# A depthwise convolution recast in eight token phases: full-width matmuls, weights spread by ScalarE, and conv tiles dealt out between GLU pieces

## The chip, the cores and the metric

The kernel runs on all 8 NeuronCores of one Trainium2 chip, two dies of four cores (0 to 3 and 4 to 7). Each core computes half the tokens of one of four batch items; the cores don't exchange data. The metric is the device time in microseconds (us) of the slowest core.

PE is TensorE (matmuls), PEld its weight loads, DVE VectorE, ACT ScalarE, POOL GpSimd, SP SyncE (here only a queue that issues DMAs).

## The reference, cut to what matters

```python
z = rms_norm(h, g_mix) @ w_in            # (B, T, 5*1024), T = 4096 + 16 meta tokens
# y_conv: the branch that the change is about
a = z[..., :1024] * sigmoid(z[..., 1024:2048])        # GLU
a = depthwise_conv(a, w_dw, width=31, centred) + b_dw # one 31-tap filter per channel
y_conv = silu(layer_norm(a, ln_g, ln_b)) @ w_conv_out # LayerNorm over all 1024 channels
# y_pool: centred window means (2, 4, 8, 16 tokens) minus the token, two matmuls
h = h + (gateA * y_conv + gateB * y_pool) @ w_o
h = h + swiglu(rms_norm(h, g_ffn))                    # 1024 -> 2816 -> 1024
out = rms_norm(h, g_final)
```

A depthwise convolution mixes tokens within a channel, whereas the conv matmuls of both kernels sum over 128 partitions (`ps<-rep_186,cw_187 128*32` in the trace of before). So both kernels bring several tokens of one channel onto different partitions. They do that by writing the GLU product to DRAM and reading it back in another arrangement.

## The kernel before

The conv stage handles 8 chunks of 128 channels. Each chunk's GLU is a pass `vg(c)` of 5 pieces of 416 tokens. The order of the passes is what the argument is about:

```python
def vg(c):                                  # one GLU pass: 80 matmuls
    for p in range(NPC):                    # NPC = 5 pieces of PW = 416 tokens
        ...                                 # 8 matmuls "gate", 8 matmuls "val"
        act(s_, bg_[:, 0:PW], AF.Sigmoid)
        tt(DVE, aT[c % 2][:, sl], bv[:, 0:PW], s_, ALU.mult)     # the GLU product
        if p == 2:
            a_out(c, 0, 3 * PW)             # SBUF -> DRAM "ad"
        pump(2)                             # two steps of the window means, on VectorE
    a_out(c, 3 * PW, EXT)

def im2col(c):                              # DRAM "ad" -> SBUF "rep": 8 loads, 4 shifted copies
    ...

def conv(c):                                # 4 tiles of 512 tokens
    for b in range(NB):
        for q in range(8):
            for j in range(4):              # 32 channels at a time, in a quarter of the array
                ...matmul(o, lhsT=lt, rhs=r_, tile_position=(0, 32 * j))
        act(d_sb[c][b][:], ps[:], AF.Identity, bias=pcc(PC_BDW, c))   # stays in SBUF
        act(dq, ps[:], AF.Square, bias=pcc(PC_BDW, c))
        ...                                 # VectorE adds to the LayerNorm sums acc_s, acc_q
    if c + 2 < KC:
        build_cw(c + 2)                     # GpSimd: the conv weights as diagonal blocks

vg(0)
im2col(0)
for c in range(1, KC):
    vg(c)
    conv(c - 1)                             # one whole GLU pass after its products
    im2col(c)
```

`nb()` hands out PSUM banks in turn, `S.dma` and `S.op` insert the semaphore waits that the data needs, and `pump(n)` issues n pieces of background work. After the loop come the gate matmuls `A(0, b)`, `conv(7)`, the LayerNorm statistics and then the rest of the block, which the change leaves alone but for the order of the tokens.

Of the kernel before, what the change touches and what calls it, by code (L numbers as in the profile page):

```python
# [13 lines left out]
KC = 8  # L14
# [9 lines left out]
HALO = 15  # L24
# [10 lines left out]
HW_ = TOK // 2  # L35
RW = HW_ + 28
RWP = 1056
THIRDS = ((0, 683), (683, 683), (1366, 682))
S_W = 704
# [5 lines left out]
(PC_BGA, PC_BGB, PC_BDW, PC_LNG, PC_LNB, PC_PSC, PC_GMIX, PC_GFFN, PC_GFIN) = range(0, 72, 8)  # L45
PC_WDW = 72
PC_COLS = PC_WDW + KC * 4 * 8
# [17 lines left out]
class Sched:  # L65
# [9 lines left out]
    def gran(self, ap):  # L75
# [17 lines left out]
        for (s, c) in dims[:-1]:  # L93
            if s == 0 or c == 1:
                continue
            offs = [o + i * s * esz for o in offs for i in range(c)]
        gs = set()
# [95 lines left out]
def build_nc():  # L193
# [18 lines left out]
    em_d = din("emask", [128, 32], BF16)  # L212
    out_d = nc.dram_tensor("out", [NB, 128, KC * TT], F32, kind="ExternalOutput")
    h1_d = nc.dram_tensor("h1d", [NB, 128, KC * TT], F32, kind="Internal")
    a_d = nc.dram_tensor("ad", [KC, 128, EXT], BF16, kind="Internal")
# [21 lines left out]
    def alloc(name, shape, dt):  # L237
# [5 lines left out]
    emask = alloc("emask_s", [128, 32], BF16)  # L243
# [10 lines left out]

    uT = at("uT", [128, KC, EXT], BF16, oA)
    psb = [at(f"psb{c}", [128, EXT], F32, oB + c * EXT * 4) for c in range(KC)]

    sqx = at("sqx", [128, KC, EXT], F32, oB)
    mT = at("mT", [128, KC, TOK], BF16, oM)
    slot = [at(f"wslot{i}", [128, 1024], BF16, oS + i * 2048) for i in range(NSLOT)]  # L260
# [3 lines left out]
    d_sb = [[at(f"d{c}_{b}", [128, TT], F32, oB + c * EXT * 4 + b * 2048) for b in range(NB)]  # L264
            for c in range(KC)]
# [4 lines left out]
    acc_s = at("acc_s", [128, TOK], F32, oW)  # L270
    acc_q = at("acc_q", [128, TOK], F32, oW + 8192)
# [7 lines left out]
    z = oZ  # L279
    aT = [at(f"aT{i}", [128, EXT], BF16, z + i * EXT * 2) for i in range(2)]  # L280
    z += 2 * EXT * 2
    rep = [at(f"rep{i}", [128, 4, RWP], BF16, z + i * 4 * RWP * 2) for i in range(2)]
    z += 2 * 4 * RWP * 2
    cw = [at(f"cw{i}", [128, 4, 8, 32], BF16, z + i * 2048) for i in range(2)]
    z += 4096
    sg = [at(f"sg{i}", [128, PW], F32, z + i * PW * 4) for i in range(2)]
    z += 2 * PW * 4
    dsq = [at(f"dsq{i}", [128, TT], F32, z + i * 2048) for i in range(2)]
    z += 4096
    s1 = at("s1", [128, S_W], F32, z)  # L290
    s2 = at("s2", [128, S_W], F32, z + S_W * 4)
    z += 2 * S_W * 4
    assert z <= oZ + NZT * 2048, (z - oZ, NZT * 2048)
# [50 lines left out]
    ad_sem = [dsem(f"d_ad{i}") for i in range(2)]  # L344
# [116 lines left out]
    for (o, i_) in ((invc[:], ic_d.ap()), (emask[:], em_d.ap())):  # L461
        S.dma(SP, cst, o, i_, val=32)
# [85 lines left out]
    def windows(c):  # L548
        g = c // 2
        wd = WINS[g]  # L550
        out = []
        for ti, (t0, n) in enumerate(THIRDS):
            lo = t0 + HALO - wd // 2
            width = n + wd - 1
            step, tgl = 1, 0
            src = psb[c][:, lo:lo + width]
            while step < wd:
                nw = width - step
                dst = (s1, s2)[tgl][:, 0:nw]
                out.append(lambda dst=dst, a=src[:, 0:nw], b=src[:, step:step + nw]:  # L560
                           tt(DVE, dst, a, b, ALU.add))
                src, width = dst, nw
                step *= 2
                tgl ^= 1
            assert width == n

            def fin(src=src, t0=t0, n=n, ti=ti):
                stt(DVE, mT[:, c, t0:t0 + n], src, 1.0 / wd, psb[c][:, HALO + t0:HALO + t0 + n],
                    ALU.mult, ALU.subtract)
                if ti == 2:  # L570
                    tt(DVE, tmp8[:], src[:, n - 8:n], invc[:, g * 8:(g + 1) * 8], ALU.mult)
                    tt(DVE, mT[:, c, TOK - 8:TOK], tmp8[:],
                       psb[c][:, HALO + TOK - 8:HALO + TOK], ALU.subtract)
                    win_done.add(c)
            out.append(fin)
        return out
# [4 lines left out]
    def build_cw(c):  # L581
        o = cw[c % 2][:].rearrange("p j q m -> p (j q) m")
        i0 = emask[:].unsqueeze(1).to_broadcast([128, 32, 32])
        ws = pc[:, PC_WDW + c * 32:PC_WDW + (c + 1) * 32]
        i1 = ws.unsqueeze(2).to_broadcast([128, 32, 32])
        S.op(POOL, lambda e: e.tensor_tensor(out=o, in0=i0, in1=i1, op=ALU.mult), [emask[:], ws], [o])

    def vg(c):
        for p in range(NPC):
            sl = slice(p * PW, (p + 1) * PW)  # L590
            bv, bg_ = nb(), nb()
            for k in range(KC):
                mm(bg_[:, 0:PW], w(f"gate{c}", k), uT[:, k, sl], k == 0, k == KC - 1)
            for k in range(KC):
                mm(bv[:, 0:PW], w(f"val{c}", k), uT[:, k, sl], k == 0, k == KC - 1)
            s_ = sg[p % 2][:]
            act(s_, bg_[:, 0:PW], AF.Sigmoid)
            tt(DVE, aT[c % 2][:, sl], bv[:, 0:PW], s_, ALU.mult)
            if p == 2:
                a_out(c, 0, 3 * PW)  # L600
            pump(2)
        a_out(c, 3 * PW, EXT)
        release(f"gate{c}", f"val{c}")

    def a_out(c, lo, hi):
        h = 0 if lo == 0 else 1
        S.dma(SP, ad_sem[h], a_d.ap()[c][:, lo:hi], aT[c % 2][:, lo:hi], xw=[("ad", c, h)])

    def im2col(c):
        for h in range(2):  # L610
            S.wait_prod(SP, ad_sem[h])
            tot = rep_sem[h].count + 16 * 4
            for s_ in range(4):
                src = a_d.ap()[c].rearrange("(j i) t -> i j t", j=4)[:, :, HW_ * h + s_:HW_ * h + s_ + RW]
                S.dma(SP, rep_sem[h], rep[h][32 * s_:32 * s_ + 32, :, 0:RW], src, val=tot)

    def conv(c):
        pump_until(win_done, c)
        for b in range(NB):
            h = b // 2  # L620
            ps = nb()
            for q in range(8):
                for j in range(4):
                    o = ps[32 * j:32 * j + 32, :]
                    lt = cw[c % 2][:, j, q, :]
                    x0 = (b % 2) * TT + 4 * q
                    r_ = rep[h][:, j, x0:x0 + TT]
                    S.op(PE, lambda e, o=o, lt=lt, r_=r_, q=q, j=j: e.matmul(  # L628
                        o, lhsT=lt, rhs=r_, start=(q == 0), stop=(q == 7), tile_position=(0, 32 * j)),
                        [lt, r_], [o], signal=(q == 7 and j == 3))  # L630
            act(d_sb[c][b][:], ps[:], AF.Identity, bias=pcc(PC_BDW, c))
            tok = slice(b * TT, (b + 1) * TT)
            dq = acc_q[:, tok] if c == 0 else dsq[b % 2][:]
            act(dq, ps[:], AF.Square, bias=pcc(PC_BDW, c))
            if c == 1:
                tt(DVE, acc_s[:, tok], d_sb[0][b][:], d_sb[1][b][:], ALU.add)
            elif c > 1:
                tt(DVE, acc_s[:, tok], acc_s[:, tok], d_sb[c][b][:], ALU.add)
            if c > 0:
                tt(DVE, acc_q[:, tok], acc_q[:, tok], dq, ALU.add)  # L640
            pump(1)
        if c + 2 < KC:
            build_cw(c + 2)

    build_cw(0)
    build_cw(1)
    vg(0)
    im2col(0)
    for c in range(1, KC):
        vg(c)  # L650
        conv(c - 1)
        im2col(c)
# [7 lines left out]
    def tile_mm(wname, rhs, weff_c=None):  # L660
        b = nb()
        for k in range(KC):
            lhsT = w(wname, k) if weff_c is None else weff[:, k, weff_c * 128:(weff_c + 1) * 128]
            mm(b[:], lhsT, rhs(k), k == 0, k == KC - 1)
        return b

    def u_rhs(b):
        return lambda k: uT[:, k, HALO + b * TT:HALO + (b + 1) * TT]

# [3 lines left out]
    def A(c, b):  # L673
        ps = tile_mm(f"gA{c}", u_rhs(b))
# [3 lines left out]
    def Bm(c, b):  # L678
        ps = tile_mm(f"gB{c}", u_rhs(b))
# [19 lines left out]
    zorder = list(range(NZT - 3, NZT)) + list(range(NZT - 3))  # L699
# [5 lines left out]
    conv(7)  # L705
# [4 lines left out]
    def ln_stat(b):  # L710
        tok = slice(b * TT, (b + 1) * TT)
# [4 lines left out]
        mm(pm[:], ones[:], acc_s[:, tok], True, True)  # L716
        mm(pq[:], ones[:], acc_q[:, tok], True, True)
        if b == NB - 1:
            var, mean, rstd = acc_q[:, tok], pm[:], psum[7][:]
# [54 lines left out]

    for g in range(4):
        wps_scale(g)
    for b in range(NB):
        A(1, b)
# [215 lines left out]
def _host_inputs(inputs):  # L994
# [12 lines left out]
    for col, v in ((PC_BGA, bg[:D]), (PC_BGB, bg[D:]), (PC_BDW, arr("b_dw")), (PC_LNG, arr("ln_g")),  # L1007
                   (PC_LNB, arr("ln_b")), (PC_PSC, arr("pool_scale")), (PC_GMIX, arr("g_mix")),
                   (PC_GFFN, arr("g_ffn")), (PC_GFIN, np.asarray(inputs["g_final"], f32))):
        pc[:, col:col + 8] = fm(v)  # L1010
    wpad = np.concatenate([arr("w_dw"), np.zeros((1, D), f32)], 0)

    pc[:, PC_WDW:] = wpad.reshape(8, 4, KC, 4, 32).transpose(1, 4, 2, 3, 0).reshape(128, KC * 32)
    emask = np.zeros((128, 32), ml_dtypes.bfloat16)
    for s_ in range(4):
# [64 lines left out]
```

## Time and profile before

| | before |
|---|---|
| time, median of its runs | 1033.8 us (1033.4 to 1035.4) |
| PE busy | 1005.6 us, 97% of the slowest core's span |
| VectorE, ScalarE, GpSimd busy | 450, 308, 158 us |
| a chunk in the conv stage | 21.2 us: 14.17 GLU, 7.02 conv |
| PE's waits for the reloaded products | 2.3 us in all |

The profiled execution itself took 1041.3 us: in it the four cores of die 1 ran at a mean clock of 0.986 to 0.990, those of die 0 at 0.995 to 0.997.

From the page of the kernel before, which is that of core 7, its slowest: the busy sums, the granted TensorE clock in tenths over 40 slices of the span, and the chain of waits that ended last, by engine. The last line is from PE's waits on the same core (total us, times, longest).

```profile
PE 1005.6 (97%) x5696; PEld 489.7 (47%) x5696; DVE 450.1 (43%) x693; ACT 307.6 (30%) x500; POOL 158.0 (15%) x182
...
PEclk9999999999989999999999999999999999999999
...
PE 91%; DMA 4%; DVE 2%; ACT 1%; issue 1%; SPq 0%; POOL 0%; DVEq 0%; ACTq 0%; POOLq 0%
...
PE ps L628 <- DMA rep_186<-ad: 2.3, 2, 1.7
```

PE is busy nearly always, and the chain that ended last runs through PE for 91% of the span. This kernel is bound by TensorE.

Two chunks of its conv stage on core 2. The columns are named in the first line; PEclk is the share of the full clock that was granted.

```profile
core 2: us, PE busy (x) PEld busy (x) DVE busy (x) ACT busy (x) POOL busy (x), PEclk, DMA share, GB/s
149.50:170.70 21.20, 21.20 (x210) 11.09 (x209) 20.38 (x30) 7.67 (x14) 6.49 (x4) 1.00 0.70 151
170.70:191.90 21.20, 21.20 (x210) 11.08 (x209) 20.41 (x30) 7.67 (x14) 6.49 (x4) 1.00 0.73 154
```

PE has work for all 21.2 us of a chunk, at full clock, and VectorE is nearly full as well (20.4 of 21.2 us).

How long the way through DRAM takes shows best in the chain of waits in order of time (core 7): start, duration, engine or DMA, what it wrote and read.

```profile
106.51 0.60 DVE aT_183 L367
107.18 6.51 DMA ad<-aT_183
...
115.09 9.29 DMA rep_186<-ad
...
124.63 3.64 PE ps L628 x64
128.27 14.17 PE ps L353 x80
142.44 7.02 PE ps L628 x128
```

After the last product of chunk 0, made by 107.1 us, the write takes 6.5 us, the reload 9.3, and its conv may start at 124.6: 17.5 us later. That costs nearly nothing, since a GLU pass of 14.17 us stands in between, and the convolution of later chunks is 21 us behind its products.

### The profile page before, as it was taken

How to read it: one execution, taken by the hardware profiler on the slowest of the kernel's cores; microseconds unless marked ns; L12 is line 12 of the kernel's file. 1: busy time of each engine (PE TensorE's matmuls, PEld its weight loads, DVE VectorE, ACT ScalarE, POOL GpSimd, SP SyncE). 2: the span in 40 equal slices, each digit the busy share in tenths (PEclk: the TensorE clock that was granted, in tenths of full speed). 3: DMA queues.
4: the chain of work that ended last, by engine and by line, in shares of the span. 5: the costliest groups of instructions: out<-in, count | busy, mean ns of one | idle time of the engine just before them, and what ended most of it. 6: DMA issues, size and time to landing. Idle time of an engine off the chain costs nothing.

```text
span 1039.7 us, 15674 instructions; the slowest of 8 cores (1026.0 to 1039.7 us)
## 1 busy us (share of the span) xinstructions
PE 1005.6 (97%) x5696; PEld 489.7 (47%) x5696; DVE 450.1 (43%) x693; ACT 307.6 (30%) x500; POOL 158.0 (15%) x182
## 2 busy tenths in 40 slices
PE   3899999999999999999999999999999999999997
PEld 1645555555434444444444444444444444444486
DVE  4542789974278532233546521212121221342454
ACT  2643333343487612211144311111111111121121
POOL 2143122221420000000167001111000000000000
PEclk9999999999989999999999999999999999999999
DMA  9705876667254111111887446655222202403112
GB/s 215 212 1 94 177 165 145 149 155 157 50 88 65 31 31 31 31 21 21 209 317 154 100 79 96 95 85 83 35 35 34 32 1 92 151 39 124 81 82 82
DMA packets 34251, 99.90 MB, mean 96 GB/s; under 512 B 3968, under 2 KB 7168, under 8 KB 31616
## 3 DMA queue, kind: packets, MB, share of 16 engines
q0 software_dynamic: 17888, 45.10, 24.6%
q1 hardware_dynamic: 16288, 53.81, 17.8%
q8 instruction: 47, 0.77, 0.3%
q14 instruction: 28, 0.23, 0.1%
HBM read 111.93 MB, written 21.04 MB: 128 GB/s over the span
## 4 chain that ended last, share of the span: by engine, by line
PE 91%; DMA 4%; DVE 2%; ACT 1%; issue 1%; SPq 0%; POOL 0%; DVEq 0%; ACTq 0%; POOLq 0%
PE ps L353 86%; PE ps L628 5%; DMA rep_186<-ad 2%; DMA xb_178<-xp 1%; DVE uT L374 1%; DMA ad<-aT_183 1%; DVE sqx L367 1%; DMA wslot_68<-w_pool_out 0%; ACT sqx L364 0%; ACT ps L364 0%; DVE h2b_259 L374 0%; ACT L364 0%; SPq L190 0%; ACT zt_197 L364 0%; ACT zt_203 L364 0%
## 5 line engine op out<-in xcount | busy, mean ns | idle before, releaser
L353 PE MATMUL ps<-mT,weff 128*128 128x512 bf16 x256 | 60.7, 386 | 0.0
L353 PE MATMUL ps<-uT,wslot_60 128*128 128x512 bf16 (+6 forms) x224 | 51.8, 356 | 5.9 <-DVE uT L374 5.3
L353 PE MATMUL ps<-uT,wslot_65 128*128 128x512 bf16 (+6 forms) x216 | 47.1, 366 | 0.0
L364 ACT ACTIVATE sgf_225<-ps 128x512 f32<-128x512 f32 x30 | 17.9, 597 | 81.3 <-PE ps L353 77.6
L364 ACT ACTIVATE sgf_226<-ps 128x512 f32<-128x512 f32 x29 | 17.3, 597 | 82.1 <-PE ps L353 82.1
L364 ACT ACTIVATE sgf_227<-ps 128x512 f32<-128x512 f32 x29 | 17.3, 597 | 79.8 <-PE ps L353 79.8
L353 PE MATMUL ps<-uT,wslot_61 128*128 128x416 bf16 (+6 forms) x192 | 40.6, 358 | 0.0
L353 PEld LDWEIGHTS ps<-mT,weff 128*128 128x128 bf16 x256 | 25.4, 99 | 31.4 <-issue 4.6
L353 PE MATMUL ps<-uT,wslot_62 128*128 128x416 bf16 (+6 forms) x192 | 39.5, 352 | 0.0
L353 PE MATMUL ps<-uT,wslot_64 128*128 128x416 bf16 (+6 forms) x192 | 38.8, 346 | 0.0
L353 PE MATMUL ps<-vT,wslot_64 128*128 128x512 bf16 x160 | 38.2, 382 | 0.0
L353 PE MATMUL ps<-vT,wslot_62 128*128 128x512 bf16 x160 | 38.2, 382 | 0.0
L353 PE MATMUL ps<-vT,wslot_67 128*128 128x512 bf16 x160 | 38.1, 380 | 0.0
L353 PE MATMUL ps<-vT,wslot_66 128*128 128x512 bf16 x160 | 38.0, 380 | 0.0
L353 PEld LDWEIGHTS ps<-uT,wslot_60 128*128 128x128 bf16 x224 | 21.8, 98 | 34.2 <-issue 16.1
L353 PE MATMUL ps<-vT,wslot_63 128*128 128x512 bf16 x160 | 37.8, 379 | 0.0
L353 PE MATMUL ps<-vT,wslot_68 128*128 128x512 bf16 x160 | 37.8, 379 | 0.0
L353 PE MATMUL ps<-vT,wslot_65 128*128 128x512 bf16 x160 | 37.8, 379 | 0.0
L353 PE MATMUL ps<-vT,wslot_61 128*128 128x512 bf16 x160 | 37.8, 379 | 0.0
L353 PEld LDWEIGHTS ps<-uT,wslot_65 128*128 128x128 bf16 x216 | 21.3, 100 | 22.5 <-issue 3.2
L353 PE MATMUL ps<-uT,wslot_68 128*128 128x416 bf16 (+1 forms) x144 | 30.9, 357 | 0.0
L353 PE MATMUL ps<-vT,wslot_60 128*128 128x512 bf16 x128 | 30.2, 379 | 0.0
(1681 smaller groups left out, 1973.7 us busy)
## 6 DMA issues: line engine op xcount, KB each, us to landing
rep_185<-ad SPq DMA_DIRECT2D x32, 263.0 KB, 6.2
rep_186<-ad SPq DMA_DIRECT2D x32, 263.0 KB, 7.5
h2b_259<-h1d SPq DMA_DIRECT2D x2, 2048.0 KB, 9.1
h1b_216<-xr POOLq DMA_DIRECT2D x1, 2048.0 KB, 14.1
h1b_217<-xr SPq DMA_DIRECT2D x1, 2048.0 KB, 15.6
h1b_218<-xr SPq DMA_DIRECT2D x1, 2048.0 KB, 19.2
h1b_219<-xr SPq DMA_DIRECT2D x1, 2048.0 KB, 24.3
h1d<-h1b_216 SPq DMA_DIRECT2D x1, 2048.0 KB, 15.3
```

The lines of the kernel that those rows point to most:

```text
L353: S.op(PE, lambda e: e.matmul(out, lhsT=lhsT, rhs=rhs, start=start, stop=stop), [lhsT, rhs], [out], signal=stop if signal is None else signal)
L364: S.op(ACT, lambda e: e.activation(out=out, in_=in_, func=func, scale=scale, **kw), reads, [out])
L367: S.op(eng, lambda e: e.tensor_tensor(out=out, in0=a, in1=b, op=op), [a, b], [out])
L374: S.op(eng, lambda e: e.scalar_tensor_tensor(out=out, in0=a, scalar=s, in1=b, op0=op0, op1=op1), [a, b] + ([] if isinstance(s, float) else ...
L628: S.op(PE, lambda e, o=o, lt=lt, r_=r_, q=q, j=j: e.matmul(o, lhsT=lt, rhs=r_, start=(q == 0), stop=(q == 7), tile_position=(0, 32 * j)), ...
```

## The change: its intent and the diff

The 128-column conv weights hold four blocks of 32 and use a quarter of the array at a time (`128*32` in the trace, where the other matmuls have `128*128`). The change arranges tokens in 8 phases (token modulo 8), so that the 128 partitions hold 16 channels by 8 phases. Then 31 taps over 8 phases span 5 shifts, and a conv tile of 2 × 256 columns is 10 full-width matmuls instead of 32 narrow ones of 512. The reload becomes one contiguous-row DMA without overlapping copies. The weights, 16 times 8 columns per block, are spread from a small table by ScalarE, which relieves GpSimd. The conv tiles are dealt out between GLU pieces, to keep PSUM and the other engines evenly loaded. In exchange the conv result comes out in (channel, phase) order and must be written to DRAM and read back, and the window means must be made of two pieces each (main and wrap). The core of the diff:

```diff
 def vg(c):
     for p in range(NPC):
         ...
-            tt(DVE, aT[c % 2][:, sl], bv[:, 0:PW], s_, ALU.mult)
-            if p == 2:
-                a_out(c, 0, 3 * PW)
-            pump(2)
-        a_out(c, 3 * PW, EXT)
+            r = (NPC * c + p) % NAT
+            tt(DVE, aT[r][:], bv[:, 0:PW], s_, ALU.mult)
+            S.dma(SP, ad_sem[r], a_d.ap()[c].rearrange("g (q h) n -> (g q) (h n)", h=NPH)[:, sl], aT[r][:])
+            pump_ex(4)
+            pump(4)
+            if c and p:
+                conv_tile(c - 1, p - 1)
         release(f"gate{c}", f"val{c}")
+        if c + 1 < KC:
+            spread(c + 1)
+        for p in range(NPC):
+            S.wait_prod(SP, ad_sem[(NPC * c + p) % NAT])
+        S.dma(SP, rep_sem[c % 2], aP[c % 2][:], a_d.ap()[c].rearrange("g p n -> p g n"))
# [cut: a_out, im2col, conv and build_cw go]
+    def spread(c):
+        S.dma(SP, tp_sem, taps[:].rearrange("p a h -> p (a h)"), tp_d.ap()[c])
+        o = cw[c % 2][:].rearrange("p g s m -> p (g s) m")
+        for q in range(16):
+            ex.append(lambda q=q: act(o[:, :, q * NPH:(q + 1) * NPH], taps[:], AF.Identity,
+                                      scale=pcc(PC_CH, q)))
+    def conv_tile(c, t):
+        if t == 0:
+            pump_until(win_done, c)
+        ps = nb()
+        for i in range(2):
+            for s_ in range(NSH):
+                mm(ps[:, i * ON:(i + 1) * ON], cw[c % 2][:, 2 * t + i, s_, :],
+                   aP[c % 2][:, 2 * t + i, s_:s_ + ON], s_ == 0, s_ == NSH - 1, ...)
+        # [cut: per half, ScalarE makes dst and the square; VectorE adds both to acc_s, acc_q]
+        S.dma(SP, dw_sem[r], dc_d.ap()[c][2 * t:2 * t + 2].rearrange("g p n -> p g n"), dst[r][:])
+        pump(1)
+    def d_back(c):
+        for r in range(3):
+            S.wait_prod(SP, dw_sem[r])
+        S.dma(SP, dr_sem[c], dall[c][:], dc_d.ap()[c].rearrange("g (q h) n -> (g q) (h n)", h=NPH))
-    build_cw(0)
-    build_cw(1)
+    spread(0)
     vg(0)
-    im2col(0)
     for c in range(1, KC):
         vg(c)
-        conv(c - 1)
-        im2col(c)
+        d_back(c - 1)
 # [cut: A(0, b)]
-    conv(7)
+    conv_tile(7, 0)
+    A(1, 0)
+    conv_tile(7, 1)
+    conv_tile(7, 2)
+    A(1, 1)
+    conv_tile(7, 3)
+    d_back(7)
# [cut: window means as main and wrap, LayerNorm statistics over phases, buffers, host layouts]
```

`ex` is a queue of ScalarE work from which `pump_ex(4)` takes four after each GLU piece. `NAT = 6` product buffers, two `aP`, two `cw`, one `taps`.

## The prediction

> **What bounds the kernel now.** TensorE. The page's busy part gives PE 1005.6 of 1039.7 us (97%); the chain of waits is 86% ordinary matmuls and 5% convolution. The conv stage (106.5 to 255.5 us) repeats every 21.2 us per channel chunk: 80 GLU matmuls in 14.17 us, then 128 conv matmuls in 7.02 us. PE waits only for DMA `rep`: 2.3 us in all. The busy-time-by-stretch view has VectorE busy 20.4 of 21.2 us from 149 to 213 us: almost a second bound.
>
> **What changes.**
> - PE: a conv tile becomes 10 matmuls of 256 columns. The last stage's 256-column matmuls start every 0.109 us, so a chunk costs 4.4 us instead of 7.05: 21 us off PE.
> - GpSimd loses 8 weight builds (29 us), which also slowed VectorE: an addition of about 690 elements took 2.08 us beside one, else 0.87.[...]
> - ScalarE gains 16 spreads per chunk, about 0.42 us each (its trace: 417 ns for 256 elements, 517 for 416), and 16 half-size evictions instead of 8: 15.4 us per chunk against 7.7, under the period.
> - VectorE: each window step becomes main plus wrap: 72 more instructions, about 0.1 us each; 24 window pieces are issued per chunk instead of 14. With 0.51 us per GLU product and 0.61 per accumulation I get 19.5 us per chunk, 22 in the two with window 16. PE needs 18.6.
> - DMA: 8 overlapping copies (2.1 MB per chunk) become one reload of 0.53 MB in 520-byte rows, plus 1 MB written and read back.
>
> **Critical path.** Before, a chunk's conv came 21 us after its last GLU matmul. Now it sits behind one conv tile and two GLU pieces: 6.8 us. Meanwhile the last product must be made (0.8 us), written to DRAM (last pieces now land 5.6 us after issue, beside weight loads; 2.2 us in quiet) and reloaded as 1024 rows[...].[...]Sum: 10 to 12 us, so PE stalls 3 to 5 us at each chunk's first conv tile. Period: 1.1 + 10.9 + 11 = 23 us, against 21.2.
>
> Seven periods: +13 us; window 16 adds 2. The end, where the last two chunks' conv shrinks, gains about 7 us after stalls of 2 us for the reload and 4 us for the statistics. Net +8: PE's 21 us are eaten by the DRAM round trip and VectorE.
>
> **Predicted: 1041 us, 1022 to 1062 (8 in 10). Faster by over 2%: 0.05; within 2%: 0.70; slower: 0.25.**
>
> **What would show it.** PE busy down about 21 us, yet idle up by 20 to 35 us, nearly all from 107 to 300 us. PE's waits: DMA `aP`, 7 or 8 times, 3 to 5 us each. 320 conv matmuls, about 35 us. VectorE busy over 85% of 107 to 250 us. ScalarE busy up about 60 us. Period 22 to 24 us. One PE wait of about 4 us for `acc_s` near 285 us.
>
> **What would make it wrong.** If write and reload take under 7 us, the stall vanishes and the period falls to VectorE's 19.5: about 1020. If the 520-byte rows take 8 us or more, or ScalarE, held by the `taps` load, delays the GLU sigmoids and so PSUM, the period passes 25 us: 1055 or more.

The sum of the round trip came to 10 to 12 us; the product's 0.8 us and the write's 5.6 leave 3.6 to 5.6 us for the reload. That GpSimd's builds slow VectorE rests on the measured additions alone: on core 7 of the kernel before one addition beside each of the four builds of 5.4 us took 2.08 to 2.09 us, others beside them 0.87. The "about 0.1 us" for each further VectorE instruction came out at 0.07: on core 2 VectorE's busy time rose by 5.8 us (450.5 to 456.3) with 86 more instructions.

## More of the kernel before

Several kernels here, the one before among them, now and then run in a slower state, in which a die or two show a lower TensorE clock: one such run of the kernel before took 1100.1 us, at mean clocks of 0.923 to 0.949 on die 0 and 0.995 to 0.999 on die 1. Such runs are marked slow and are left out of every comparison. A run in which only a pair of cores shows a lower clock (0.957 to 0.960 in three of the change's runs) still counts as fast; where that matters it is said.

## The result, and the profile after

| | before | after |
|---|---|---|
| time, median of 4 fast runs each | 1034.1 us | 1077.5 us (1070.7 to 1080.1) |
| ratio of fast runs | 1 | 1.0408 (95%: 1.0359 to 1.0457), slower |
| PE busy (slowest core) | 1005.6 us, 97% | 1002.7 us, 93% |
| PE busy, core 2 | 992.7 us | 987.0 us |
| ScalarE busy | 307.6 us | 383.3 us |
| core 2: span | 1026.6 us | 1060.8 us |

A ratio is the mean time of one kernel's fast runs over the mean of the other's fast runs of the same rounds, so it is not quite the ratio of the medians that stand beside it.

The page of the kernel after, that of core 4, the same parts, and two of its costly groups (busy us, mean ns of one, then the idle time before them and what ended most of it):

```profile
PE 1002.7 (93%) x4947; PEld 505.6 (47%) x5008; DVE 456.8 (42%) x779; ACT 383.3 (36%) x694; POOL 125.4 (12%) x174
...
PEclk9999888778878999999999999999999999999999
...
PE 81%; DMA 8%; ACT 4%; DVE 4%; issue 3%; DVEq 0%; POOL 0%; ACTq 0%; SPq 0%; POOLq 0%
...
L382 ACT ACTIVATE cw<-taps_s,pc_s 128x320 bf16<-128x320 f32 x128 | 71.8, 561 | 36.5 <-DMA taps_s<-taps 27.3
L371 PE MATMUL ps<-aP,cw 128*128 128x256 bf16 x320 | 49.0, 311 | 35.6 <-DMA aP<-ad 29.0
```

By the weight loads there are 688 fewer matmuls (5696 − 5008; some matmul records are missing from this trace), and yet PE is busy almost as long. The clock line says why: in slices 5 to 13, which are the conv stage, the granted clock reads 7 and 8 tenths, where the kernel before shows 9 in all but one. Core 4 is one of a pair with a further slow clock, of which more below; core 2, which is free of it, shows the dip too:

```profile
PEclk9999889899989999999999999999999999999998
```

And before the 320 conv matmuls PE stood idle for 35.6 us on core 4, 29.0 of them for `aP`, the reload.

Three chunks on core 2, each from one first conv tile to the next:

```profile
core 2: us, PE busy (x) PEld busy (x) DVE busy (x) ACT busy (x) POOL busy (x), PEclk, DMA share, GB/s
144.47:168.34 23.87, 19.98 (x120) 12.24 (x121) 15.70 (x34) 14.67 (x34) 1.05 (x2) 0.93 0.58 158
168.34:192.86 24.52, 20.00 (x121) 12.25 (x122) 19.28 (x41) 17.71 (x40) 1.05 (x2) 0.92 0.61 168
192.86:218.62 25.76, 21.38 (x121) 12.74 (x122) 18.57 (x40) 16.93 (x38) 1.06 (x2) 0.89 0.53 149
```

A chunk takes 24 to 26 us instead of 21.2. No engine is busy all that time: VectorE for 15.7 to 19.3 us, ScalarE for 14.7 to 17.7. PE is busy for 20 to 21.4 us, where the work at full clock is 14.17 + 4 × 1.10 = 18.6.

PE's waits on core 2 (total us, times, longest):

```profile
PE ps L371 <- DMA aP<-ad: 36.3, 8, 7.2
...
PE ps L371 <- DVE acc_s L385: 3.4, 1, 3.4
```

All eight chunks wait for the reload. (On other cores the same view names ScalarE's weights `cw` or a window step for one to three of the stalls. By the times it was the reload there, too: on every core each of the eight first conv tiles starts 0.1 to 0.3 us after its reload has landed, and the last spread of its weights had ended at least 9.8 us before.) One such stall in PE's timeline on core 2 (start, us, what, count; in brackets the idle time just before and what ended it):

```profile
182.55 5.79 PE L371 MATMUL ps<-uT,wslot 128*128 128x416 bf16 x32
192.86 2.29 PE L371 MATMUL ps<-aP,cw 128*128 128x256 bf16 x10 [4.51 <-DMA aP<-ad]
194.94 4.75 PE L371 MATMUL ps<-uT,wslot 128*128 128x416 bf16 x16
199.52 1.26 PE L371 MATMUL ps<-aP,cw 128*128 128x256 bf16 x10
200.62 2.98 PE L371 MATMUL ps<-uT,wslot 128*128 128x416 bf16 x16
```

The first conv tile can't start until 192.86, 4.51 us after the GLU pieces before it. And look at what follows: that tile takes 2.08 us from its start to the next group's (192.86 to 194.94), the next tile 1.10 (199.52 to 200.62). The GLU piece behind the stall takes 4.58 us, the later one 2.8. The whole stretch from 192.86 to 199.52 is 6.66 us, where a tile and a piece at full clock take 3.91. The same core in slices of 3 us:

```profile
189.00:192.00 3.00, 0.00 (x0) 0.00 (x0) 0.31 (x1) 2.72 (x6) 0.00 (x0) 0.95 0.97 247
192.00:195.00 3.00, 2.14 (x11) 1.56 (x12) 2.60 (x5) 2.05 (x4) 0.00 (x0) 0.50 0.88 346
195.00:198.00 3.00, 3.00 (x10) 1.31 (x9) 1.56 (x4) 1.56 (x4) 0.00 (x0) 0.50 0.21 72
198.00:201.00 3.00, 3.00 (x21) 1.98 (x20) 1.28 (x4) 2.37 (x5) 0.00 (x0) 0.91 0.10 29
```

The third number from the end is the clock. After the stall it is 0.50 for two slices; only then does it come back. The other stalls show the same: after the first seven, of 2.63 to 7.24 us, core 2 worked for 2.7 to 5.7 us at 0.50. Whether the idle time is what brings the clock down this trace alone doesn't show; e3 and e8 test it. The prediction had no such term.

Why the reload lands so late shows in the SP queue's timeline on core 2 (DMA issues in their order):

```profile
183.23 0.32 SPq L199 DMA_DIRECT2D ad<-aT  x1
184.14 0.37 SPq L199 DMA_DIRECT2D dcd<-dst  x1
184.60 0.42 SPq L199 DMA_DIRECT2D taps_s<-taps  x1
188.16 0.37 SPq L199 DMA_DIRECT2D aP<-ad  x1
```

The last product's write leaves at 183.23. The reload must wait until it has landed, and leaves at 188.16, 4.9 us later. It lands at 192.6, another 4.5 us. Together 9.4 us, while the two GLU pieces that hide it last about 5.6.

ScalarE's waits on the same core between 95 and 310 us show a second new wait, for the table of taps:

```profile
ACT cw L382 <- DMA taps_s<-taps: 28.7, 7, 5.0
```

There is one `taps` buffer. Its load may start only when the last spread of the chunk before has read it, and the next spread, at the head of ScalarE's queue, waits for it. The GLU's sigmoid stands behind it: in the stall shown ScalarE waited 4.15 us for the taps, until 189.00, and the sigmoid `sg` started at 191.42, after four spreads.

Last, the cores differ (span and mean granted clock of each):

```profile
core 2: 1060.8 us, clock 0.976
...
core 4: 1076.5 us, clock 0.957
core 5: 1068.8 us, clock 0.958
```

On cores 4 and 5 a third value of the clock appears, 0.81 in this slice of core 4:

```profile
237.00:240.00 3.00, 3.00 (x20) 1.93 (x19) 3.00 (x5) 2.65 (x5) 0.00 (x0) 0.81 0.25 87
```

It holds on this pair from 181 to about 340 us, but for the half-clock spells in between. In two other of the four runs one pair has a mean clock of 0.957 to 0.960 as well; in the fourth (1070.66 us) none has. Going by that one run, it adds roughly 7 us to the reported time and would explain most of the spread between runs.

### Where core 2's 34.2 us come from

I split the span at the last GLU product of chunk 0 (at 106.1 us in both), at that of chunk 7, and at the first pooled matmul (`mT`).

| core 2 | before | after | difference |
|---|---|---|---|
| seven passes: product of chunk 0 to product of chunk 7 | 141.3 | 173.3 | +32.0 |
| from there to the first pooled matmul | 58.3 | 60.6 | +2.3 |
| rest | 720.9 | 720.8 | 0 |

In the passes after stand seven GLU passes and 27 conv tiles (the 28th comes behind the last product), so the work at full clock is 7 × 14.17 + 27 × 1.10 = 128.9 us, and the first seven waits for `aP` sum to 32.8 (6.41, 7.24, 3.88, 4.51, 4.38, 2.63, 3.79). That leaves 173.3 − 128.9 − 32.8 = 11.6 us, 1.7 per chunk, for work at half clock. The trace's clock record agrees: behind these stalls PE worked for 24.3 us at 0.50, and half of that is 12.2.

### The profile page after: what moved, and what is told of

It is laid out like the page before. It is cut to its first block, busy times and chain, and to the rows that moved or that the text cites. A ratio compares the mean times of both kernels' runs of the same rounds, so it can differ in the third digit from the quotient of the medians.

```text
span 1076.5 us, 14790 instructions; the slowest of 8 cores (1060.8 to 1076.5 us)
## 1 busy us (share of the span) xinstructions
PE 1002.7 (93%) x4947; PEld 505.6 (47%) x5008; DVE 456.8 (42%) x779; ACT 383.3 (36%) x694; POOL 125.4 (12%) x174
## 3 DMA queue, kind: packets, MB, share of 16 engines
q1 hardware_dynamic: 29712, 58.82, 15.7%
## 4 chain that ended last, share of the span: by engine, by line
PE 81%; DMA 8%; ACT 4%; DVE 4%; issue 3%; DVEq 0%; POOL 0%; ACTq 0%; SPq 0%; POOLq 0%
PE ps L371 81%; DMA aP<-ad 3%; DMA ad<-aT 3%; ACT cw L382 1%; DMA xb<-xp 1%; DVE uT L392 1%; DMA taps_s<-taps 1%; DVE sb L385 1%; DVE sqx L385 1%; DMA wslot<-w_pool_out 1%; DVE aT L385 1%; ACT dsq L382 0%; ACT dst L382 0%; DVE mT L392 0%; ACT sqx L382 0%
## 5 line engine op out<-in xcount | busy, mean ns | idle before, releaser
L371 PE MATMUL ps<-uT,wslot 128*128 128x416 bf16 (+6 forms) x1536 | 319.2, 365 | 6.1 <-DVE uT L392 5.4
L371 PE MATMUL ps<-vT,wslot 128*128 128x512 bf16 x1380 | 302.9, 379 | 1.5
L371 PEld LDWEIGHTS ps<-uT,wslot 128*128 128x128 bf16 x1536 | 155.5, 102 | 156.3 <-issue 34.7
L371 PEld LDWEIGHTS ps<-vT,wslot 128*128 128x128 bf16 x1408 | 137.7, 98 | 167.0 <-issue 1.6
L385 DVE TENSOR_TENSOR fT<-ps,sgf 128x512 bf16<-128x512 f32 x88 | 60.7, 692 | 229.1 <-PE ps L371 229.1
L371 PE MATMUL ps<-fT,wfd 128*128 128x512 bf16 (+1 forms) x869 | 152.6, 336 | 0.6
L371 PEld LDWEIGHTS ps<-fT,wfd 128*128 128x128 bf16 x880 | 86.1, 98 | 67.8 <-issue 1.7
L382 ACT ACTIVATE zt<-ps,pc_s 128x512 f32<-128x512 f32 x64 | 43.4, 688 | 123.5 <-PE ps L371 121.1
L382 ACT ACTIVATE cw<-taps_s,pc_s 128x320 bf16<-128x320 f32 x128 | 71.8, 561 | 36.5 <-DMA taps_s<-taps 27.3
L371 PE MATMUL ps<-aP,cw 128*128 128x256 bf16 x320 | 49.0, 311 | 35.6 <-DMA aP<-ad 29.0
L371 PE MATMUL ps<-act,wslot 128*128 128x512 bf16 x254 | 59.1, 379 | 0.1
L371 PEld LDWEIGHTS ps<-aP,cw 128*128 128x128 bf16 x320 | 34.5, 109 | 50.5 <-issue 39.8
L371 PE MATMUL ps<-mrg,wslot 128*128 128x512 bf16 x251 | 55.5, 379 | 0.3
L382 ACT ACTIVATE dst<-ps,pc_s 128x256 f32<-128x256 f32 x64 | 30.2, 472 | 31.7 <-PE ps L371 31.3
```

The costliest lines, as they stand in the source:

```text
L371: S.op(PE, lambda e: e.matmul(out, lhsT=lhsT, rhs=rhs, start=start, stop=stop), [lhsT, rhs], [out], signal=stop if signal is None else signal)
L382: S.op(ACT, lambda e: e.activation(out=out, in_=in_, func=func, scale=scale, **kw), reads, [out])
L385: S.op(eng, lambda e: e.tensor_tensor(out=out, in0=a, in1=b, op=op), [a, b], [out])
```

## The experiments

Four theories stood against each other. The round trip: PE stalls because the products aren't back from DRAM when the first conv tile comes, and then runs at half clock. The taps: ScalarE, held by the taps load, delays the sigmoids, hence the products and PSUM. The clock itself: the full-width conv matmuls, rather than the stalls, bring it down. VectorE: its longer window pieces set the pace. In the expectations T1 is the round trip, T2 the taps and ScalarE; what the further numbers stand for is said where they are used.

Times below are of fast runs; each ratio is against the kernel before in the same rounds.

### e1_late: conv tiles two GLU pieces later

```diff
-            if c and p:
-                conv_tile(c - 1, p - 1)
+            if c and p > 2:
+                conv_tile(c - 1, 2 * p - 6)
+                conv_tile(c - 1, 2 * p - 5)
```

The work is the same, but the first tile comes after piece 3, so four pieces (11.3 us) hide the round trip instead of two.

> Edit: the four conv tiles of a chunk stand after GLU pieces 3 and 4 (two each) of the next pass instead of after pieces 1 to 4; nothing else. T1 (the DRAM round trip of the GLU products stalls PE 5 to 7 us per chunk, and each stall halves the granted clock for some us): the tiles now have about 11.3 us of GLU work ahead of them besides the previous conv tile against a round trip of 11 to 13 us, so PE waits for aP fall from 29 to 36 us to under 10 us, the 0.50 clock spells vanish, the time falls by 30 to 45 us to 1032 to 1047 us. T2 (ScalarE waiting for taps delays the products): little changes, over 1065 us. T3 (the full-width conv matmuls lower the clock by themselves): the waits go but the clock in the conv stage stays under 0.95, 1045 to 1055 us. T4 (VectorE limits the period at 19.5 to 22 us): waits on aP turn into waits on VectorE, 1035 to 1045 us.

Measured: 1044.6 to 1046.2 us, ratio 1.0110 (1.0093 to 1.0127); one more run was slow. By order alone 32 of the 43 us of loss are gone, or 25 of 37 against the change's one run without the 0.81 clock, which no fast run of e1 shows. PE's waits on core 2:

```profile
PE ps L371 <- ACT dsq L382: 11.9, 8, 2.9
...
PE ps L371 <- DMA aP<-ad: 3.2, 1, 3.2
```

The eight waits for the reload became one, and the mean clocks of the cores, which lay between 0.957 and 0.978, now lie between 0.984 and 0.995. A new wait took its place: `dsq`, ScalarE's eviction of the conv tiles. ScalarE still waits for the taps (24.0 us, 7 times). The half-clock spells did not vanish, though I had expected it: between 100 and 360 us core 2 has 10.2 us of them, where the change has 41.0. (By the time alone, the branch in which the full-width matmuls lower the clock would fit as well; that branch has it under 0.95 in the conv stage, and from 100 to 300 us it is 0.95 to 0.98 on the eight cores. e3 and e8 decide this more clearly.)

### e2_taps: two taps buffers

```diff
-    taps = at("taps_s", ...)
+    taps = [at("taps_s0", ...), at("taps_s1", ...)]      # room for it: NAT = 5 instead of 6
 def spread(c):
-        S.dma(SP, tp_sem, taps[:]..., tp_d.ap()[c])
+        if c + 1 < KC:
+            taps_load(c + 1)                              # one chunk ahead
```

> Edit: two taps buffers, each loaded one whole chunk ahead (and 5 instead of 6 product buffers, for room). T2: the ScalarE waits for taps (27 us) go, sigmoids come earlier, the period falls by 2 to 4 us, 1050 to 1062 us. T1: these waits lie inside PE's stall on aP, so the time moves by less than 8 us: 1069 to 1080 us, with PE's waits for aP still 25 us or more.

Measured: 1075.1, 1069.2, 1068.0 and 1066.6 us, ratio 1.0346 (1.0305 to 1.0387), slower; about 6 us better than the change (1.0408 − 1.0346 of 1034), but the two intervals overlap. A part of that may be the 0.81 state, which one of these four runs showed and three of the change's: e2's three runs without it are 1.5 to 4 us below the change's one. ScalarE's wait for the taps is gone from its list, yet PE's stands on core 2:

```profile
PE ps L371 <- DMA aP<-ad: 36.0, 8, 6.0
```

So the taps were a real wait, but not the one that holds PE.

### e3_fill: useless matmuls before the first conv tile

```diff
         if t == 0:
             pump_until(win_done, c)
+        if t == 0 and c < KC - 1:
+            for n in range(NFILL):                        # NFILL = 40
+                mm(psum[7][:, 0:256], w(f"val{c + 1}", n % KC), uT[:, n % KC, 0:256], True, True, ...)
```

Forty matmuls, about 4.4 us, fill the time in which PE would wait, into a bank that nobody reads. If idle time brings the clock down, this makes the kernel faster by adding work. If the conv's own load did, it would make it slower.

> Edit: 40 matmuls of 256 columns on data long there, results unused, put in front of the first conv tile of each of seven chunks, about 4.4 us of extra PE work where PE waits anyway. If the half clock after a stall is caused by PE's idling, [...]the 0.50 spells go, and the time falls although work was added: by 8 to 15 us, to 1062 to 1069 us. If the low clock has another cause (T3: full-width conv; the die's state), the spells stay and the time is the same or up to 10 us longer.

Measured: 1058.8 to 1063.9 us, ratio 1.0264 (1.0232 to 1.0296); one more run was slow. About 15 us faster than the change, with some 31 us (7 × 4.4) of PE work added. (Against the change's one run without the 0.81 state, which no fast run of e3 shows, it is still 7 to 12 us.) On core 2 the same place now reads:

```profile
179.53 10.16 PE L372 MATMUL ps<-uT,wslot 128*128 128x416 bf16 x72
189.84 1.26 PE L372 MATMUL ps<-aP,cw 128*128 128x256 bf16 x10 [0.16 <-issue]
190.94 2.98 PE L372 MATMUL ps<-uT,wslot 128*128 128x416 bf16 x16
```

(The first group counts the fillers too.) There is no wait, the conv tile takes 1.10 us, the piece behind it 2.8, and core 0's clock is 1.00 from 90 to 276 us. (In the whole trace core 2 still waits for `aP` five times, 8.9 us in all, 3.8 at the longest.) The half clock was the price of the stalls, not of the conv matmuls.

### e4_olddata: the reload takes chunk 0's data (wrong result)

```diff
-        for p in range(NPC):
-            S.wait_prod(SP, ad_sem[(NPC * c + p) % NAT])
-        S.dma(SP, rep_sem[c % 2], aP[c % 2][:], a_d.ap()[c]...)
+        if c == 0:
+            for p in range(NPC):
+                S.wait_prod(SP, ad_sem[(NPC * c + p) % NAT])
+        S.dma(SP, rep_sem[c % 2], aP[c % 2][:], a_d.ap()[0]...)
```

The same DMA, but it needn't wait for this chunk's writes to land; it reads what landed long ago. The result is wrong (relative error 0.38).

> Wrong result on purpose. Edit: every reload takes the products of chunk 0 and so waits for no write of its own chunk; size, rows and place of the reload stay. It measures the write's share of the round trip. T1: the reload is issued about 3 us after the last GLU matmul instead of 8, lands about 5 us earlier, so the stall falls from 5 to 7 us to 0 to 2 us, no 0.50 spells, 1030 to 1045 us. If the reload in 520-byte rows alone is the limit: stalls of 3 us or more stay, over 1055 us.

Measured: 1059.2 to 1064.3 us, ratio 1.0269 (1.0227 to 1.0312); one more run was slow. A miss: I had expected 1030 to 1045. The write is half of the trip, but the other half is enough to stall PE:

```profile
PE ps L371 <- DMA aP<-ad: 21.9, 6, 4.5
```

(core 4; core 2 14.6 us, 6 times.) On core 0 the reload was now issued at 182.92 us, behind a `dcd` write and the taps load in the same queue, where PE was ready for it at 186.0; it lands 6.4 us after its issue. Over all cores the 64 reloads took 6.1 us in the median, where the change's took 4.8, so the edit also made them longer. Reload and its place in the queue alone are longer than what hides them.

### e5_late_taps: e1 and e2 together

> Edit: the late conv tiles of e1_late and the two taps buffers of e2_taps together. In e1_late the chain of waits ran through the taps load (27 us of ScalarE waiting) and ScalarE's spreads once the round trip was off it. If that is the next limit, both together gain 6 to 15 us over e1_late: 1030 to 1039 us, with ScalarE's waits for taps under 3 us. If VectorE (19.5 to 22 us per chunk) or the conv result's write (dst buffers) is the limit, it stays at 1042 to 1047 us.

Measured: 1025.9 to 1027.8 us, ratio 0.9941 (0.9925 to 0.9957): better than the range that I had given. The second taps buffer is worth about 6 us in the change, not clear of the noise, and about 17 us (1.0110 − 0.9941 of 1034) once the round trip is hidden. The two limits stood one behind the other, so neither's worth could be read while the other stood. The taps line is gone from ScalarE's waits on core 2, and the list (95 to 285 us) now begins with a wait for PE's conv tiles:

```profile
ACT dst L382 <- PE ps L371: 11.8, 10, 4.7
```

### e6_deal: the tiles dealt out across two passes

```diff
-            if c and p:
-                conv_tile(c - 1, p - 1)
+            if p < 2 and c > 1:
+                conv_tile(c - 2, p + 2)
+            if p == 3 and c > 1:
+                d_back(c - 2)
+            if p > 2 and c:
+                conv_tile(c - 1, p - 3)
+            if p == 1 and c:
+                spread(c)
# and the two taps buffers of e2; the last tiles of chunk 6 between the A(0, b);
# chunk 7: A(1, 0), two tiles, A(1, 1), two tiles
```

It keeps one tile per piece, as the change meant it, but starts after piece 3, so that chunk c's tiles reach into the next pass.

> Edit: a chunk's four conv tiles are dealt one each after pieces 3 and 4 of the next GLU pass and pieces 0 and 1 of the one after it; the spreads and the read-back move along; two taps buffers. The round trip has 11.3 us of GLU pieces plus two conv tiles (13.5 us) to hide in. T1: no PE wait for aP over 2 us, clock 0.99, period 19 to 21 us, 1010 to 1030 us, so faster than before the change or level with it. If evenness of the tiles does not matter: as e5_late_taps within 4 us.

Measured: 1024.5 to 1025.8 us, ratio 0.9926 (0.9908 to 0.9944); one more run was slow. The clock is 1.00 throughout the passes (on all cores, to 250 us); what remains of PE's waits lies mostly at the end of the stage (core 1):

```profile
PE ps L371 <- DVE acc_s L385: 6.9, 1, 6.9
...
PE ps L371 <- DMA aP<-ad: 3.1, 2, 2.8
```

### e7_deal_pump: fewer window pieces per GLU piece

e6 with `pump(4 - p % 2)` instead of `pump(4)`, which takes VectorE work out of the passes and leaves it for later.

> Edit: e6_deal with 22 instead of 24 window pieces issued per chunk (the rest come in the last pass, which had none). If VectorE limits e6_deal's period, each chunk gains about 1 us: 4 to 8 us less than e6_deal. If ScalarE or PE limits it: within 2 us of e6_deal.

Measured: 1026.2 to 1029.1 us, ratio 0.9942 (0.9925 to 0.9958), against e6's 0.9926: the intervals overlap, so nothing was gained in all. But the traces show that VectorE does set the pace of the fifth period at least. From one first conv tile to the next, PE's own time is about 18.45 us: no period is shorter but the last, and many are just that. On cores 0 to 3 the fifth takes 20.2 to 21.4 us in e6 and 18.5 in e7; the window pieces put off then come in the last pass, whose period grows on two of these cores (from 16.3 to 22.0 us on core 0).

### e8_before_early: the kernel before, with its convolution too early

```diff
 def vg(c):                      # in the kernel BEFORE
             tt(DVE, aT[c % 2][:, sl], bv[:, 0:PW], s_, ALU.mult)
+            if p == 1 and c:
+                conv(c - 1)
             if p == 2:
         ...
         vg(c)
-        conv(c - 1)
         im2col(c)
```

If the early place of the convolution is the cause, the kernel before must lose by it too, though its matmuls are the narrow ones.

> Edit to the kernel BEFORE: its conv of a chunk (32-column matmuls) stands after GLU piece 1 of the next pass instead of behind the whole pass, so PE must wait about 6 to 10 us per chunk for rep. If idling is what halves the granted clock, whatever the matmul's width, spells of 0.50 of 3 to 7 us appear after each wait in this kernel too, and the time goes to 1085 to 1125 us. If the full-width conv matmuls are needed for the low clock (T3): the clock stays 0.99 and only the waits add, 1075 to 1100 us.

Measured, one run: 1108.6 us beside 1033.2, all cores at mean clocks of 0.967 to 0.975. Seven waits for `rep` on core 2, 50.5 us, the longest 8.7, and behind each the half clock, here with the old matmuls of 32 columns:

```profile
237.00:240.00 3.00, 0.00 (x0) 0.00 (x0) 0.00 (x0) 0.00 (x0) 0.00 (x0) 0.50 1.07 219
240.00:243.00 3.00, 2.51 (x24) 1.09 (x28) 0.00 (x0) 0.00 (x0) 0.00 (x0) 0.50 0.88 181
243.00:246.00 3.00, 3.00 (x33) 1.30 (x29) 1.01 (x2) 1.27 (x2) 0.00 (x0) 0.50 0.07 17
246.00:249.00 3.00, 3.00 (x60) 1.59 (x56) 2.44 (x6) 1.46 (x3) 0.00 (x0) 0.95 0.00 0
```

So neither stalls nor half clock need the phases, the full-width matmuls, or ScalarE's weights. They follow from where the convolution stands. (It is worse here than in the change, where core 2 waits 36.3 us in all for the reload. The reload here is eight copies of 263 KB (in the trace of before) instead of one of 520 KB; that this is the reason, no run tests.)

### e9_tail: chunk 7's tiles after one gate tile, three gate tiles behind them

e6, with `A(1, 0)`, then all four tiles of chunk 7, then `A(1, 1)` to `A(1, 3)` ahead of the LayerNorm statistics, so that 5 us of matmuls hide the sums' way to PE.

> Edit: e6_deal with the four gate tiles A(1,0..3) all placed ahead of the LayerNorm statistics instead of two of them between the statistics. In e6_deal PE waits 6.9 us for acc_s there and restarts at 0.50 to 0.70 of the clock for about 9 us. With 5.3 us of gate tiles in that place the wait shrinks to under 3 us and the cold spell goes: 4 to 8 us less than e6_deal, 1017 to 1021 us. If the end of the stage is limited by ScalarE or VectorE instead: within 2 us of e6_deal.

Measured: 1024.9 and 1024.4 us, ratio 0.9906 (0.9889 to 0.9924). Only two of its eight runs were fast, so this rests on two. A miss: 1017 to 1021 expected, and the intervals of e6 and e9 overlap. The wait for `acc_s` went, and others showed (core 2):

```profile
PE ps L371 <- DMA aP<-ad: 4.0, 3, 2.6
...
PE ps L371 <- ACT zt L382: 1.9, 1, 1.9
```

### e10_two_spreads: weights spread for two chunks only (wrong result)

e9, with the 16 spreads for chunks 0 and 1 only; later chunks convolve with those weights (relative error 0.35). It takes 96 of 128 spreads off ScalarE and nothing else.

> Wrong result on purpose. Edit: e9_tail with the ScalarE spreads made for chunks 0 and 1 only (96 of 128 activations gone, 0.63 us from start to start each, so about 10 us per chunk off ScalarE). If ScalarE limits the repaired conv stage, it shrinks by 4 to 12 us more; if PE or VectorE does, the time stays within 2 us of e9_tail.

Measured: 1020.9 to 1023.3 us, ratio 0.9877 (0.9864 to 0.9890), against e9's 0.9906: about 3 us, which the two fast runs of e9 barely resolve. That lies between the two branches of the expectation. Once the taps are loaded ahead, ScalarE's spreads, three quarters of which are gone here, cost little.

### e11_pool_queue: the result's DMAs in another queue

```diff
-        S.dma(SP, dw_sem[r], dc_d.ap()[c][2 * t:2 * t + 2]..., dst[r][:])
+        S.dma(POOL, dw_sem[r], dc_d.ap()[c][2 * t:2 * t + 2]..., dst[r][:])
 def d_back(c):
-            S.wait_prod(SP, dw_sem[r])
-        S.dma(SP, dr_sem[c], dall[c][:], ...)
+            S.wait_prod(POOL, dw_sem[r])
+        S.dma(POOL, dr_sem[c], dall[c][:], ...)
```

On top of e9, the writes and read-backs of the conv result leave from GpSimd's queue, so the products and the reload don't stand behind them.

> Edit: e9_tail with the conv result's writes and read-backs issued from the GpSimd queue instead of the sync queue, where they stand in line behind the waits of the reload. In e6_deal the chain of waits shows 10 us and 7 us on a dcd write. If that in-order queue matters: 2 to 6 us less than e9_tail. If not, or if issuing from GpSimd costs as much as it saves: within 2 us of e9_tail, or slower.

Measured: 1024.4, 1021.9 and 1023.3 us, ratio 0.9886 (0.9869 to 0.9904); one more run was slow. It is the fastest kernel with a right result: 1.1% faster than the kernel before, 5% faster than the change. Its interval lies below 1. That it beats e9 is not shown; the intervals overlap.

## Why the prediction was wrong

The prediction was 1041 us, range 1022 to 1062, with 0.25 on slower; the kernel takes 1077.5. Point by point:

**Right: PE bound before, and what the change would stall on.** The waits for `aP`, 8 of them, the longest 7.2 us; the wait for `acc_s`, 3.4 us where about 4 was said. Even the size of the stalls was right: the period of 1.1 + 10.9 + 11 = 23 us holds a stall of 4.4 us, and seven of them with the 2 us for window 16 make 32.8. Core 2 measured 32.8; that it agrees to the decimal is luck, since the five other cores without the 0.81 clock have 31.7 to 37.0. The parts fit too: last product's write until the reload's issue 4.9 us in the stall shown (5.6 was said for the landing), reload 4.5 (4.0 to 6.6 over the eight; the sum left 3.6 to 5.6 for it).

**The step that failed: "Period: 1.1 + 10.9 + 11 = 23 us, against 21.2" and, built on it, "Seven periods: +13 us".** It failed in two ways: a cost was missing, and the sum was wrong.

- It has no term for the clock. The GLU and conv work behind each stall was costed at full speed, while it ran at half clock for 2.7 to 5.7 us. Core 2's period was 24.7 us, not 23: 1.7 us more per chunk, 11.6 in seven passes, and another 3.4 in the last part (the first conv tile of chunk 7, the gate tile behind it and the first statistics took 9.7 us where they take 6.3 at full clock). e3 shows the cause: filling the stalls with useless matmuls brings the clock back (means of 0.989 to 0.996 on the eight cores, where the change has 0.957 to 0.978) and up to 15 us with it. e8 shows that it needs nothing of the change but the stall. The same term made the prediction of PE's busy time fail: down 21 us was said, 5.7 was measured on core 2, because the slow work counts as busy (21 less the 15 us of half clock leaves 6). And the conv matmuls were busy for 46.0 us on core 2, not 35; of the difference about 5 us are only the way of counting (a tile at full clock counts 1.26 us of busy time, though the next work starts after 1.10).
- Its bookkeeping counted one convolution twice. "Seven periods" at 21.2 us put seven convolutions into the passes of the kernel before, but its first pass has none behind it: the seven passes take 14.17 + 6 × 21.2 = 141.4 us (141.3 measured). The next step, "The end, where the last two chunks' conv shrinks, gains about 7 us", then took two more out, nine of eight. With its own terms the passes were to lose 7 × 23 + 2 − 1.1 − 141.3 = 20.6 us (1.1 for the conv tile that comes behind the last product) and the end to gain 2.7 (two convolutions of together 14.2 out, five tiles of 5.5 and waits of 6 in): a net +18, not +8. The sum done right would have been about 1052 us, still inside the range; the missing clock term alone, 11.6 + 3.4 us, takes it out of it.

| core 2, us | |
|---|---|
| net change that the prediction stated | +8 |
| its sum done right, on top of that | +10 |
| half clock behind the stalls in the passes | +11.6 |
| half clock at the end | +3.4 |
| more waits at the end than predicted, and rounding | +1.2 |
| measured | +34.2 |

(The "half clock" terms are what remains after work at full clock and waits, so they are worked out, not read.)

**What the account of core 2 doesn't hold.** The reported time rose by 43.4 us, the slowest core's, not core 2's. About 7 us of the rise probably belong to the pair of cores at clock 0.81: the one run in which no pair was slowed took 1070.7 us. That state showed in three of four runs of the change, and in some of e2 and e4, which keep the stalls and the full-width matmuls. No other kernel's fast runs show a pair so far below the rest. But neither the stalls nor the full-width matmuls are needed for this clock: the profiled execution of the kernel before has it on all four cores of die 1, in spells of 4 to 10 us that add up to 39 us on cores 4 and 5 and 53 us on cores 6 and 7. Nor do dense matmuls on all cores suffice for it: in the change's profile every core runs at 1.00 from 341 to 1050 us, with PE busy for over 99% of that time, and only a pair of cores had fallen to 0.81, while the other two of their die stayed out of it (in e2's profile both pairs of die 1 fell). What sets it off stays open.

**ScalarE: mis-sized and then misjudged.** Busy time rose by 76 us, not 60: a spread took 0.56 us, one started every 0.65 (median), and not 0.42. The estimate came from activations with no per-partition operand, though in the trace of before the activations with such an operand, there a bias, already took 0.688 us where those without took 0.597 (512 elements). The prediction named the taps load as a risk. It was 28.7 us of waits for ScalarE, but hidden behind the reload: worth about 6 us alone (e2, not clear of the noise) and 17 us with the round trip gone (e5).

**VectorE: not the bound in the change, but the next one in part.** "VectorE busy over 85% of 107 to 250 us" was said, 73% measured on core 2 (104.5 of 143.0 us). It was also said that without the stall "the period falls to VectorE's 19.5: about 1020". With the trip hidden, e5 to e11 come to 1021 to 1029, so that estimate of the change's worth was close, with some luck: in e6 the first four periods take 18.45 to 19.5 us on cores 0 to 3, at or near PE's own time, and only the fifth, of up to 21.4 us, was shown to go at the pace of VectorE's window pieces (e7). The gain was there, and it was spent on the order of the tiles.

**Rejected and open.** Rejected as the main cause: the taps alone (e2), the full-width conv matmuls (e3, e8), VectorE (e1 and e5 leave its work as it was). Shown: the distance between the products and the first conv tile (e1, e5, e6 one way, e8 the other). Open: what sets off the 0.81 state, and whether e9's end or e11's queue gain anything, since the differences lie inside the intervals.

## What to carry to other kernels

Place the consumer of a DRAM round trip further behind its producer than write, issue and reload together, each read from the trace with its place in the queue: here 9.4 us in the stall shown, and moving the first conv tile back by two pieces of work was worth 32 us of 43 (25 of 37 without the 0.81 clock). Cost a TensorE stall of a few us as the stall plus a restart at half clock, here 1.7 us more on average for each stall of 2.6 to 7.2. Shorter gaps should be costed, too, for every second one of 2 to 3 us was followed by the half clock. The shortest in view: a wait of 2.63 us on core 2 in the kernel after (clock 0.50 from 242.9 us), one of 2.61 us on core 2 in e9 (0.50 from 254.3), and one of 1.84 us on core 0 in the kernel before (0.50 from 294.6). Counted over all cores of the 13 kept traces, from 100 to 1000 us of the span, such a spell began by 3.6 us after the end of none of 265 waits of PE of 0.5 to 1.5 us, 13 of 188 of 1.5 to 2, 41 of 82 of 2 to 3, 104 of 121 of 3 to 4, and all 191 of more than 4. (Waits that began at half clock are left out. The traces of before and after alone give 0 of 15, 3 of 22, 4 of 6, 16 of 19 and 42 of 42.) And when a change adds two waits, test them together as well as apart: the second was worth about 6 us while the first stood, and 17 after it.
